# Each column block of the up projection reads its weight parts from another place inside 512 bytes

## The chip, the cores and the metric

The kernel runs on one core of a Trainium2 chip. The metric is device time in microseconds (us) of one execution. Engines are named as the profile names them: PE is TensorE's matrix multiply, PEld its loading of the stationary operand, DVE is VectorE, ACT is ScalarE, POOL is GpSimd, and SP issues most of the DMAs.

## What is computed

One decoder layer over 256 tokens of width 2048: a combined input projection, two parallel branches (a gated DeltaNet and a block-sparse attention), an output projection, and then a gated MLP with a causal convolution of width 3 behind its up projection. The change touches the up projection, `h @ w_up`, alone:

```python
D_MODEL = 2048
SEQ = 256
D_FF = 5632
...
    x = x + merged @ w_out[l]
    h = rms_norm(x, ln2[l])
    u = causal_dwconv(h @ w_up[l], ffn_conv[l], ffn_conv_bias[l])
    u_gate, u_val = jnp.split(u, 2, axis=-1)
    x = x + (jax.nn.silu(u_gate) * u_val) @ w_down[l]
return rms_norm(x, final_norm)
```

## The kernel before

**Split arithmetic.** All large products are made in a 32-bit format of TensorE called fp32r here, with each operand split into a high and a low part. For a weight tile, ACT casts the float32 original `wraw` to the high part `wh` (line 108, in `split`), and DVE subtracts it from the original to get the low part `wl` (line 105, in `low`). The activations are split once in the same way. Three products are kept: high by high, low by high and high by low.

**Weight buffers.** `fetch` (line 116) has SP load one 1 MB piece of weights, 128 partitions by 2048 float32, into one of four `wraw` buffers. `load_w` (line 125) makes both parts of it in two pieces of 1024 columns each. `parts` (line 121) hands out the buffers `wh` and `wl`, two of each. Each is 2048 + 128 elements wide, and its argument `o` says at which element the 2048 that are used begin. With `o` at 0 a part starts at the buffer's own start. `SHIFT` (line 30) is 72 elements, 288 bytes.

**Two kinds of product.** `chunk` and `block` (lines 160 to 180) use the weights as the stationary operand and the activations as the moving one; they serve the DeltaNet's projections (`ps_gdn`) and the output projection (`ps_wo`, whose activations `mc` are shifted by `SHIFT` too), with `o` at 0. `by_token` (line 182) does it the other way round: a 128 by 128 block of the activations is the stationary operand, loaded before each matmul, and 512 columns of `wh` or `wl` are the moving operand. It serves `ps_z`, `ps_v`, `ps_moba`, `ps_gate`, `ps_br` and the up projection, `ps_up`, all with `parts(SHIFT)`. The down projection (`pd`, line 987) also moves the weights, with `o` at 0; its last two weight pieces lie in the tile `tail` (line 985), which takes the memory that `hc` and `h2` had.

**The up projection** (line 964) goes over 22 blocks of 512 columns. Each block loads four pieces of weights, and each piece feeds 24 matmuls of 512 columns: two halves of the tokens, four slices of the contraction, three products. That is 96 matmuls for a block and 2112 for the stage. The stationary operand is `h2`, the normed activations, in the memory of the tile tagged `hc`. Behind each block, ACT moves the sums out of PSUM (line 968), and the transposing and convolving of it (`convolved`, line 943) is done in small steps between the matmuls of the blocks that follow.

**Addresses.** In the built program each `wraw`, `wh` and `wl` buffer begins 192 bytes past a multiple of 512, in every partition, and so do the down projection's activation parts `ah` and `al`. `hc`, `h2` and `tail` begin 480 bytes past one. Blocks and slices inside these tiles are multiples of 512 bytes apart, so the place inside 512 bytes is the same for each matmul of a stage. With `SHIFT` the moving operand of the up projection begins at 192 + 288 = 480.

Of the kernel before, what the change touches and what calls it, by code (L numbers as in the profile page):

```python
# [22 lines left out]
KD = D // P  # L23
# [4 lines left out]
EPS = 1e-6  # L28
EVERY = 1700
SHIFT = 72  # L30
ATT_SCALE = 128 ** -0.5
CONST_FIELDS = [
    ("ident", 128), ("nm", 128), ("my", 2 * 64), ("nm3", 3 * 128), ("invf", 16),
# [37 lines left out]
def layer_kernel(ctx: ExitStack, tc: tile.TileContext, xT, pos, cst, ceye, vec, convw, ffw, bdv,  # L71
# [8 lines left out]
    def r3(t, b):  # L80
        return t.rearrange("p (a b) -> p a b", b=b)
# [15 lines left out]
    def main_mm(ps, a, b, start, stop):  # L97
        pe.matmul(ps, a, b, start=start, stop=stop, skip_group_check=True)  # L98
        spent[0] += 215 if b.free_size() > T else 108
        if spent[0] >= EVERY:  # L100
            spent[0] = 0
            tick()
# [4 lines left out]
    def split(hi, lo, src):  # L107
        casts.append(act.copy(hi, src))  # L108
        return low(hi, lo, src)
# [6 lines left out]
    def fetch(src, n=2048):  # L116
        raw = wpool.tile([P, 2048], F32, name="wraw", tag="wraw", bufs=4)
        sp.dma_start(raw[:, :n], src)
        return raw

    def parts(o=0):

        return [wpool.tile([P, 2048 + 128], F32R, name=t, tag=t)[:, o:o + 2048] for t in ("wh", "wl")]

    def load_w(src, n=2048, into=None, piece=1024, raw=None):
        raw = raw or fetch(src, n)
        wh, wl = into or parts()
        for o in range(0, n, piece):
            lows.append(split(wh[:, o:o + piece], wl[:, o:o + piece], raw[:, o:o + piece]))
        return wh[:, :n], wl[:, :n]  # L130
# [23 lines left out]
    def mmt(name):  # L154
        return pst[0].tile([P, 2, 2, T] if wide[0] else [P, 2, T], F32, name=name, tag="mm")
# [15 lines left out]
    def chunk(blocks, x, kt, name, raws=(None, None), piece=1024, steps=((0, 0, None), (1, 0, None)), flush=None):  # L171
        ps = mmt("ps_" + name)
        ws = {}
        for n, (j, k0, k1) in enumerate(steps):
            while n == flush and bg:
                tick()
            if j not in ws:
                ws[j] = load_w(blocks[j], kt * P, raw=raws[j], piece=piece)
            block(ps[:, j], ws[j], x, kt, k0, k1)
        return ps  # L180

    def by_token(ws, x, kt, name):

        if wide[0]:
            t = mmt(name)
            ps = [t[:, i].rearrange("p a b -> p (a b)") for i in range(2)]
        else:
            ps = [mmt(name).rearrange("p a b -> p (a b)") for _ in range(2)]
        for q_ in range(kt // 4):
            wh, wl = (r3(t, 512) for t in load_w(ws[q_], into=parts(SHIFT)))  # L190
            for i in range(2):
                s = slice(i * P, (i + 1) * P)
                for k in range(4):
                    a = q_ * 4 + k
                    main_mm(ps[i], x[:, a, 0, s], wh[:, k, :], a == 0, False)
                    main_mm(ps[i], x[:, a, 1, s], wh[:, k, :], False, False)
                    main_mm(ps[i], x[:, a, 0, s], wl[:, k, :], False, a == kt - 1)
        return ps
# [476 lines left out]
    def pair(w, i):  # L675
        return [w[2 * i], w[2 * i + 1]]

    def z_gates(n):
        ps = by_token(w_z[4 * n:4 * n + 4], hc, KD, "ps_z")
        zv = ya[:, 4 * n:4 * n + 4, :].rearrange("p (a b) c -> p a b c", b=2)  # L680
        for i in range(2):
            act.activation(zv[:, :, i, :], r3(ps[i], T), AF.Silu, scale=cols[:, 5 + i, 0:1])

    v4 = []
    for n in range(2):
# [4 lines left out]
        for pr in range(2):  # L690
# [3 lines left out]
            for a, t in enumerate((kq[:, 1], kq[:, 0], v)):  # L694
                if gr == 0 and a < 2:
                    ps = (ps_q0, ps_k0)[a]
                else:
                    ps = chunk(pair(w_gdn, 3 * gr + a), hc, KD, "gdn")
# [9 lines left out]
        if n == 0:  # L708
            bg.append(rotary())

            for c in range(2):
                ps = by_token(w_mv[4 * c:4 * c + 4], hc, KD, "ps_v")
                v4.append(m.tile([P, 2, 2 * T], F32, name="v_"))
                for i in range(2):
                    act.mul(v4[c][:, i, :], ps[i], cols[:, 5 + i, 0:1])
# [18 lines left out]
    def moba(h0, q, k, v):  # L734
        ss = []
        for j in range(2):
# [8 lines left out]
            dve.tensor_reduce(mx[:, 1:2], s_[:, T:], axis=AX.X, op=ALU.max)  # L745
            dve.tensor_scalar(mx[:, 0:2], mx[:, 0:2], -ATT_SCALE, None, op0=ALU.mult)
            act.activation(s_[:, :T], s_[:, :T], AF.Exp, bias=mx[:, 0:1], scale=ATT_SCALE, accum_out=mx[:, 2:3])
            act.activation(s_[:, T:], s_[:, T:], AF.Exp, bias=mx[:, 1:2], scale=ATT_SCALE, accum_out=mx[:, 3:4])
            dve.reciprocal(mx[:, 2:4], mx[:, 2:4])
# [35 lines left out]
    for n in range(2):  # L785
        if n:
            while ("pair", 1, 1) not in done:
                tick()
            gdn_st.close()
            mq = mq_st.enter_context(tc.tile_pool(name="mq", bufs=1, reuse_waits="tile"))  # L790
        qks.append([])
        for a in range(2):
            ps = by_token(w_moba[8 * n + 4 * a:8 * n + 4 * a + 4], hc, KD, "ps_moba")
            t = (m if a else mq).tile([P, 4, 2, P], F32, name=f"qk{a}", bufs=1)
            for i in range(2):
                act.activation(t[:, :, i, :], r3(ps[i], P), AF.Identity, scale=cols[:, 5 + i, 0:1])
            qks[n].append(t)
            bg.append(rotated(t, ("qk", n, a)))

    gts = []  # L800
    for c in range(8):
        ps = by_token(w_gate[4 * c:4 * c + 4], hc, KD, "ps_gate")
# [28 lines left out]
    m = m_st.enter_context(tc.tile_pool(name="mp", bufs=1, reuse_waits="tile"))  # L831
    mc = m.tile([P, KD * 2 * T + 128], F32R, name="mc")[:, SHIFT:SHIFT + KD * 2 * T].rearrange("p (k a t) -> p k a t", a=2, t=T)

# [32 lines left out]
    for c in range(4):  # L866
        ps = by_token(w_ba[2 * c:2 * c + 2], yc[0], H, "ps_br")
# [3 lines left out]
        ps = by_token(w_bb[2 * c:2 * c + 2], yc[1], H, "ps_br")  # L871
# [15 lines left out]
    h2 = hp.tile([P, KD, 2, T], F32R, name="h2", tag="hc")  # L887
    for c in range(8):
        if c == 0:
            steps = ((0, 0, 8), (0, 8, 12), (1, 0, 4), (0, 12, KD), (1, 4, KD))  # L890
            ps = chunk(pair(w_o, c), mc, KD, "wo", steps=steps, flush=1)
# [5 lines left out]
        else:  # L897
            ps = chunk(pair(w_o, c), mc, KD, "wo")
# [44 lines left out]
    def convolved(n, ut):  # L943
        c, val = n // 2, n % 2
        uc = ub.tile([P, 4, T], F32, name="uc", bufs=2)
        yield from turn(r3(uc.rearrange("p k t -> p (k t)"), P), ut.rearrange("p k i c -> p (k i c)"),
                        ub.tile([P, 8, P], F32, name="xt"), sp, 4, 1)
        yield from wait(5)
        if not val:
            gates[c] = ub.tile([P, 4, T], F32, name="sgt", bufs=2)  # L950
        for k in range(4):
            ch = 4 * c + k
            if val:
                t = ub.tile([P, T], F32, name="cvf", bufs=2)
                conv3(t, uc[:, k, :], NF + ch)
                pool.tensor_tensor(acts[:, ch, :], gates[c][:, k, :], t, op=ALU.mult)  # L956
            else:
                conv3(gates[c][:, k, :], uc[:, k, :], ch)
            yield
        if not val:  # L960
            act.activation(gates[c], gates[c], AF.Silu)

    bg.append(residual_turned())
    for n in range(NF // 2):
        ps = by_token(w_up[4 * ((n % 2) * 11 + n // 2):][:4], h2, KD, "ps_up")
        ut = ub.tile([P, 4, 2, P], F32, name="ut", bufs=2)
        for i in range(2):
            act.activation(ut[:, :, i, :], r3(ps[i], P), AF.Identity, scale=R2c[:, i:i + 1])
        bg.append(convolved(n, ut))
# [14 lines left out]
    wl = {}  # L984
# [8 lines left out]
    for k in range(NF):  # L993
# [10 lines left out]
        wh, wl_ = load_w(w_dn[k], into=[tail[:, t, k - NF + 2, :] for t in range(2)] if k >= NF - 2 else None)  # L1004
# [98 lines left out]
```

## Time and profile before

| | |
|---|---|
| median of three runs (lowest, highest) | 1464.84 us (1463.58, 1468.98) |
| span of the profiled execution, first to last instruction | 1464.6 us |
| mean granted TensorE clock | 0.998 |
| up projection: first to last matmul of `ps_up` | 731.9 to 1214.2 us |
| down projection: first to last matmul of `pd` | 1214.4 to 1456.5 us |
| bytes moved by DMA in the span | 297.43 MB |
| landing of one 1 MB piece of `w_up`, median | 7.4 us |

The page of the profile has the busy time of each engine, the span in 40 slices, the chain of work that ended last and the costliest groups of instructions. In a group's row stand the line, the engine, the operation, the tiles written and read, the shapes and the count, then its busy time and the mean length of one in ns, then the idle time of the engine ahead of it and what ended that. Matmuls overlap: the length of one runs from its start to its modelled end, and the next begins before that. The distance from one start to the next is read from the timeline. Rows of the tiles `ps_up`, `pd` and `ps_wo` belong to the stages named above, since a tile's name is that of its stage.

### The profile page before, as it was taken

To read this page: it belongs to the slowest core of one execution; us is meant where nothing else is said; L and a number is where in the kernel's file an instruction comes from. 1 tells how busy PE (TensorE), PEld (TensorE's weight loads), DVE (VectorE), ACT (ScalarE), POOL (GpSimd) and SP (SyncE) were. 2 spreads that over 40 slices of the span, in tenths; PEclk is the share of its full clock that TensorE was granted. 3 is DMA by queue.
4 is the path that set the end of the run, shared out by engine and by line. 5 is a ranking of instruction groups with operands and counts; after the bars stand their busy time and mean duration, and the time that the engine had idled before them with its cause. 6 is when DMAs were issued, how large, how long until landed. Compare 5 with 4: busy or idle time off the path is not lost.

```text
span 1464.6 us, 19064 instructions
## 1 busy us (share of the span) xinstructions
PE 1449.5 (99%) x7193; PEld 1228.0 (84%) x7193; DVE 957.7 (65%) x1358; ACT 737.1 (50%) x944; POOL 132.5 (9%) x121
## 2 busy tenths in 40 slices
PE   8999999999999999999999999999999999999997
PEld 8898899888887888888888888888888887888886
DVE  7987876888455445767656576576676666654554
ACT  5665444645375434445446455455455555444444
POOL 0011000200003000001100122210011111000000
PEclk9999999999999999999999999999999999999999
DMA  9566554577535555676557677777687776555552
GB/s 323 175 217 213 181 190 142 151 238 238 185 117 187 196 184 200 210 266 229 181 173 235 172 252 223 191 252 226 183 255 219 211 229 218 204 199 198 183 194 86
DMA packets 206252, 297.43 MB, mean 203 GB/s; under 512 B 167272, under 2 KB 169712, under 8 KB 174032
## 3 DMA queue, kind: packets, MB, share of 16 engines
q1 hardware_dynamic: 185952, 288.27, 60.4%
q10 hardware_dynamic: 18128, 4.20, 1.5%
q0 software_dynamic: 2080, 3.75, 0.7%
q8 instruction: 56, 0.92, 0.3%
q14 instruction: 36, 0.29, 0.1%
HBM read 273.54 MB, written 3.15 MB: 189 GB/s over the span
## 4 chain that ended last, share of the span: by engine, by line
PE 73%; DMA 11%; SPq 7%; DVE 6%; ACT 1%; issue 1%; POOLq 0%; ACTq 0%; DVEq 0%; POOL 0%
PE pd L98 16%; PE ps_gate L98 11%; PE ps_up L98 10%; PE ps_gdn L98 8%; DMA wraw<-in_w_up 8%; SPq L464 7%; PE ps_wo L98 6%; PE ps_moba L98 6%; PE ps_br L98 6%; DVE wl L105 3%; PE ps_z L98 3%; PE ps_v L98 3%; DMA uc<-xt 2%; DVE sgt L939 2%; DMA wraw<-in_w_gdn 1%
## 5 line engine op out<-in xcount | busy, mean ns | idle before, releaser
L105 DVE TENSOR_TENSOR wl<-wraw,wh 128x1024 fp32r<-128x1024 f32 x496 | 603.0, 1251 | 278.2 <-ACT wh L108 277.8
L108 ACT CAST wh<-wraw 128x1024 fp32r<-128x1024 f32 x496 | 495.3, 1046 | 423.3 <-PE ps_up L98 139.8
L98 PE MATMUL ps_up<-wh,h 128*128 128x512 f32 x1408 | 433.8, 389 | 0.0
L98 PEld LDWEIGHTS ps_up<-wh,h 128*128 128x128 f32 x1408 | 264.3, 188 | 54.5
L98 PE MATMUL ps_up<-wl,h 128*128 128x512 f32 x704 | 275.0, 391 | 0.3 <-DVE wl L105 0.2
L98 PE MATMUL ps_gate<-wh,hc 128*128 128x512 f32 x512 | 158.4, 394 | 1.3 <-ACT wh L108 1.3
L98 PEld LDWEIGHTS ps_up<-wl,h 128*128 128x128 f32 x704 | 132.1, 188 | 30.8 <-DVE wl L105 3.2
L98 PE MATMUL pd<-wl,ah 128*128 128x512 f32 x336 | 129.7, 390 | 0.5 <-DVE wl L105 0.5
L98 PE MATMUL pd<-wh,al 128*128 128x512 f32 x336 | 129.2, 389 | 0.0
L98 PE MATMUL ps_gdn<-hc,wh 128*128 128x256 f32 x704 | 125.6, 281 | 0.0
L98 PEld LDWEIGHTS ps_gate<-wh,hc 128*128 128x128 f32 x512 | 96.5, 189 | 21.3 <-ACT wh L108 1.7
L956 POOL TENSOR_TENSOR acts<-sgt,cvf 128x256 f32<-128x256 f32 x44 | 68.7, 1579 | 451.6 <-ACT wh L108 284.4
L98 PEld LDWEIGHTS ps_gdn<-hc,wh 128*128 128x128 f32 x704 | 108.0, 188 | 0.3
L98 PE MATMUL ps_gdn<-hc,wl 128*128 128x256 f32 x352 | 98.6, 280 | 0.7 <-DVE wl L105 0.7
L98 PE MATMUL ps_gate<-wl,hc 128*128 128x512 f32 x256 | 98.3, 394 | 0.4 <-DVE wl L105 0.4
L98 PE MATMUL pd<-wh,ah 128*128 128x512 f32 x336 | 93.0, 390 | 0.5 <-DVE pd L981 0.4
L98 PE MATMUL ps_wo<-mc,wh 128*128 128x512 f32 x256 | 89.2, 391 | 0.2 <-DVE mc L864 0.2
L98 PE MATMUL ps_moba<-wh,hc 128*128 128x512 f32 x256 | 77.8, 390 | 0.0
L98 PEld LDWEIGHTS pd<-wh,ah 128*128 128x128 f32 x336 | 62.9, 188 | 14.8 <-ACT wh L108 0.9
L98 PEld LDWEIGHTS pd<-wl,ah 128*128 128x128 f32 x336 | 63.1, 188 | 14.0 <-DVE wl L105 0.9
L98 PEld LDWEIGHTS pd<-wh,al 128*128 128x128 f32 x336 | 63.1, 188 | 13.1
L108 ACT CAST ah<-acts 128x256 fp32r<-128x256 f32 x44 | 17.7, 406 | 109.5 <-PE pd L98 104.4
(428 smaller groups left out, 1704.9 us busy)
## 6 DMA issues: line engine op xcount, KB each, us to landing
wraw<-in_w_up SPq DMA_DIRECT2D x88, 1024.0 KB, 7.4
wraw<-in_w_dn SPq DMA_DIRECT2D x44, 1024.0 KB, 4.9
wraw<-in_w_gate SPq DMA_DIRECT2D x32, 1024.0 KB, 5.0
wraw<-in_w_gdn SPq DMA_DIRECT2D x22, 1024.0 KB, 5.0
wraw<-in_w_moba SPq DMA_DIRECT2D x16, 1024.0 KB, 5.6
wraw<-in_w_o SPq DMA_DIRECT2D x16, 1024.0 KB, 5.5
uc<-xt SPq DMA_DIRECT2D x352, 32.0 KB, 2.0
wraw<-in_w_z SPq DMA_DIRECT2D x8, 1024.0 KB, 6.4
```

The lines of the kernel that those rows point to most:

```text
L98: pe.matmul(ps, a, b, start=start, stop=stop, skip_group_check=True)
L105: return (eng or dve).tensor_tensor(lo, src, hi.bitcast(F32), op=ALU.subtract)
L108: casts.append(act.copy(hi, src))
L464: eng.dma_start(dst[32 * e:32 * e + 32, :, 32 * a:32 * a + 32], xt[32 * a:32 * a + 32, :, 32 * e:32 * e + 32])
L939: dve.scalar_tensor_tensor(t[:, d:], u[:, :T - d], w[:, 2 - d:3 - d], t[:, d:], op0=ALU.mult, op1=ALU.add)
L956: pool.tensor_tensor(acts[:, ch, :], gates[c][:, k, :], t, op=ALU.mult)
```

## The change

A table `PLACES` of 22 shifts replaces the one shift of 72 elements in the up projection: block `n` takes entry `n`. The first sixteen are multiples of 8 elements (32 bytes) from 0 to 120, that is, each place in steps of 32 bytes inside 512 once; the last six are 2, 4, 70, 74, 76 and 12 elements (8, 16, 280, 296, 304 and 48 bytes). Entry 9 is 72, as before. All other uses of `by_token` keep `SHIFT`.

```diff
 SHIFT = 72
+PLACES = (0, 8, 16, 24, 32, 40, 48, 56, 64, 72, 80, 88, 96, 104, 112, 120, 2, 4, 70, 74, 76, 12)
...
-    def by_token(ws, x, kt, name):
+    def by_token(ws, x, kt, name, shift=SHIFT):
...
-            wh, wl = (r3(t, 512) for t in load_w(ws[q_], into=parts(SHIFT)))
+            wh, wl = (r3(t, 512) for t in load_w(ws[q_], into=parts(shift)))
...
-        ps = by_token(w_up[4 * ((n % 2) * 11 + n // 2):][:4], h2, KD, "ps_up")
+        ps = by_token(w_up[4 * ((n % 2) * 11 + n // 2):][:4], h2, KD, "ps_up", PLACES[n])
```

The order of instructions on every engine, what each of them waits for, and the base address of every buffer are the same in both built programs. What differs is the address at which ACT and DVE write, DVE reads and TensorE reads the parts of the weights in the up projection, and, from line 31 on, the line numbers by one.

## The prediction

> **What bounds the kernel now.** I read the page first: the busy shares, the slices, the chain that ended last and the costliest groups.
>
> ```profile
> PE 1449.5 (99%) x7193; PEld 1228.0 (84%) x7193; DVE 957.7 (65%) x1358; ACT 737.1 (50%) x944; POOL 132.5 (9%) x121
> PE   8999999999999999999999999999999999999997
> PEclk9999999999999999999999999999999999999999
> PE 73%; DMA 11%; SPq 7%; DVE 6%; ACT 1%; issue 1%; POOLq 0%; ACTq 0%; DVEq 0%; POOL 0%
> L105 DVE TENSOR_TENSOR wl<-wraw,wh 128x1024 fp32r<-128x1024 f32 x496 | 603.0, 1251 | 278.2 <-ACT wh L108 277.8
> L108 ACT CAST wh<-wraw 128x1024 fp32r<-128x1024 f32 x496 | 495.3, 1046 | 423.3 <-PE ps_up L98 139.8
> ```
>
> TensorE is busy for 99% of the span at a full granted clock, and the engines that prepare its weights wait for it: ACT's cast sits idle 139.8 us until a ps_up matmul frees a buffer. So the span is set by how often TensorE can start a matmul. Then I asked for the stage that the change touches: the instructions on the tile ps_up, the waits of TensorE between 732 and 1214 us, and the sums of that stretch.
>
> ```profile
> L98 PE MATMUL ps_up<-wh,h x1408: 387/389/475, 731.9 to 1214.0; 128*128 128x512 f32 x176
> L98 PE MATMUL ps_up<-wl,h x704: 387/389/505, 732.5 to 1214.2; 128*128 128x512 f32 x176
> PE ps_up L98 <- DVE wl L105: 0.2, 1, 0.2
> 732.00:1214.00 482.00, 481.67 (x2122) 396.65 (x2122) 316.58 (x373) 256.20 (x320) 62.11 (x40) 1.00 0.72 216
> ```
>
> The up projection is 1408 + 704 = 2112 matmuls of 512 columns between 731.9 and 1214.2 us, 482.3 us, a third of the span. TensorE waits 0.2 us in it for anything the profile names. Here each nanosecond per matmul is worth 2.1 us, nearly all of it on the path.
>
> The durations (389 ns) overlap, so what counts is the distance from start to start. It is read from the timeline of TensorE: its columns are start in us, length in us, and how many were merged into the row.
>
> ```profile
> 1100.13 0.39 PE L98 MATMUL ps_up<-wl,h 128*128 128x512 f32 x1
> 1100.36 0.62 PE L98 MATMUL ps_up<-wh,h 128*128 128x512 f32 x2
> ...
> 1104.89 0.39 PE L98 MATMUL ps_up<-wl,h 128*128 128x512 f32 x1
> ```
>
> From 1100.13 to 1104.89 lie 21 starts: 4.76 / 21 = 226.7 ns. 2112 of these make 478.7 us, so all but 3.6 us of the stage is this one steady step. It isn't the only step that the same instructions at the same addresses take. Just after a short wait it is another:
>
> ```profile
> 1074.46 0.64 PE L98 MATMUL ps_up<-wh,h 128*128 128x512 f32 x2
> 1074.93 0.40 PE L98 MATMUL ps_up<-wl,h 128*128 128x512 f32 x1
> 1075.16 0.62 PE L98 MATMUL ps_up<-wh,h 128*128 128x512 f32 x2
> ...
> 1077.24 0.62 PE L98 MATMUL ps_up<-wh,h 128*128 128x512 f32 x2
> ```
>
> From 1074.46 to 1077.24 are 12 starts in 2.78 us, 231.7 ns each; then the 226.7 sets in. So a stream of matmuls settles after a disturbance, and before it has settled a matmul costs 5.0 ns more. The change asks whether the place of the moving operand decides about this.
>
> **The change, part by part.** No instruction is added, removed or reordered on any engine, and no wait and no DMA; the buffers keep their base addresses and size. What moves is the start of wh and wl inside their padded buffers, in the up projection alone. The built program has all of these buffers 192 bytes past a multiple of 512, and h2, which TensorE loads as the stationary operand, 480 past. With 72 elements (288 bytes) the moving operand starts at 480 too: **the same place inside 512 bytes as the stationary one**. After the change that holds for block 9 alone. Blocks 18, 19 and 20 (70, 74, 76) lie 8 to 16 bytes from it, and the other 18 blocks 32 to 256 bytes, counted round the 512.
>
> *ACT and DVE, which write and read at the new places.* Two stages of the trace have these buffers at 192 and at 480: the down projection (first two rows) and the branch projections (last two).
>
> ```profile
> L105 DVE TENSOR_TENSOR wl<-wraw,wh 128x1024 fp32r<-128x1024 f32 x55 | 65.0, 1221 | 14.8 <-ACT wh L108 14.8
> L108 ACT CAST wh<-wraw 128x1024 fp32r<-128x1024 f32 x56 | 56.0, 1047 | 0.0
> L105 DVE TENSOR_TENSOR wl<-wraw,wh 128x1024 fp32r<-128x1024 f32 x26 | 30.9, 1218 | 17.4 <-ACT wh L108 17.4
> L108 ACT CAST wh<-wraw 128x1024 fp32r<-128x1024 f32 x26 | 26.0, 1047 | 42.0 <-PE ps_br L98 42.0
> ```
>
> 1221 against 1218 ns and 1047 against 1047 ns: their place costs nothing. The cover is large as well: a load feeds 24 matmuls, 24 x 226.7 = 5.44 us, against two DVE pieces of 1.22 and two casts of 1.05. At 8 bytes past a 16 (places 2, 70 and 74) no row shows them; even doubled they fit (4.9 of 5.44 us). I cost it at nothing; without that cover, three blocks of four loads would lose at most what DVE takes beyond 5.44 us.
>
> *TensorE.* What the trace has of a moving and a stationary operand at different places are two stages, both with the moving one at 480 and the stationary one at 192, 288 bytes apart. The first is the end of the down projection, where the tile tail takes turns with wh and wl (which lie at 192):
>
> ```profile
> 1441.49 0.63 PE L98 MATMUL pd<-tail,ah 128*128 128x512 f32 x2
> ...
> 1442.89 0.39 PE L98 MATMUL pd<-wl,ah 128*128 128x512 f32 x1
> ...
> 1443.36 0.62 PE L98 MATMUL pd<-tail,ah 128*128 128x512 f32 x2
> ...
> 1444.75 0.40 PE L98 MATMUL pd<-wl,ah 128*128 128x512 f32 x1
> ...
> 1445.21 0.62 PE L98 MATMUL pd<-tail,ah 128*128 128x512 f32 x2
> ...
> 1446.61 0.40 PE L98 MATMUL pd<-wl,ah 128*128 128x512 f32 x1
> ```
>
> Six tail matmuls (rows of 2, 1, 2 and 1) take 1.40, 1.39 and 1.40 us: 4.19 / 18 = 232.8 ns, 6.1 over the settled step. The second is the output projection, which alternates 512 and 256 columns:
>
> ```profile
> 679.81 0.39 PE L98 MATMUL ps_wo<-mc,wh 128*128 128x512 f32 x1
> 680.04 0.28 PE L98 MATMUL ps_wo<-mc,wl 128*128 128x256 f32 x1
> ...
> 683.97 0.39 PE L98 MATMUL ps_wo<-mc,wh 128*128 128x512 f32 x1
> ```
>
> Twelve pairs in 4.16 us: 346.7 ns, 120.0 more than one settled 512-column matmul. If a column costs 0.417 ns and each matmul 13.3 ns besides (0.417 x 512 + 13.3 = 226.7), the pair comes to 0.417 x 768 + 26.7 = 346.7: no loss at all. So the two nearest rows bound the cost of a place that doesn't match at **0 and +6.1 ns**. Below zero the bound comes from a stream that reloads its weights as often and shows no such surplus, the plain f32 matmuls near the start:
>
> ```profile
> 15.20 4.05 PE L261 MATMUL ps_gdn<-xs,wraw 128*128 128x256 f32 x18
> 10.85 3.69 PE L261 MATMUL ps_gdn<-xs,wraw 128*128 128x256 f32 x16 [0.15 <-DVE hc L214]
> L261 PE MATMUL ps_gdn<-xs,wraw 128*128 128x256 f32 x64 | 14.8, 384 | 2.1 <-DMA xs<-in_xT 1.9 <-DVE hc L214 0.2
> ```
>
> (4.05 - 0.38) / 17 = 215.9 ns from start to start, with 384 ns for the last one: a lower end of -10.8 ns, for another number format, so far off.
>
> I take +5.0 ns, the step of the stream that hasn't settled. The tail is the nearest row (same columns, format and line), but each of its runs is six long and begins with a change of place, while a settling takes about a dozen; its 232.8 may be a little too high for a block of 96. For the three places within 16 bytes of 72 I take nothing. **Sum: 18 blocks x 96 matmuls x 5.0 ns = 8.6 us.** The chance waits of DVE (part of the 3.6 us) are as likely to grow as to shrink with a slower TensorE. The profiled span is 1464.6 us and the median of the three runs 1464.84, so the two can be taken as one: 1464.84 + 8.6 = **1473.5 us**, +0.6%.
>
> **The rivals.**
>
> *The place makes no difference; not slower.* Mechanism: the step is a matter of time alone. It settles whenever moving and stationary reads come in a fixed rhythm, wherever they lie. For it: the output projection, 288 bytes apart and without loss; and in the down projection both operands lie at 192, at 480 in the up projection, with the same settled step. The tail would then be slow because its moving operand jumps between 192 and 480, not because it stands apart from ah. Each block would pay one settling at most, 2.78 - 12 x 0.2267 = 0.06 us, 21 times 1.3: 1464.8 to 1466.1. It decides if settled blocks appear at 32 to 256 bytes of distance. The Trainium skill's page "TensorE: Matmul & The Clock Gate", section "What happens when you issue a matmul", gives this rival a reason: TensorE reads the moving operand and the weights through two ports of their own, and loading the next weights takes nothing from the running matmul. By it the sum would be nothing, 1464.8; the tail's 232.8 beside 226.7 speaks against it, the output projection's 346.7 for it.
>
> *Some places settle and some don't.* If half of the 18 find the 226.7 again: 9 x 96 x 5.0 = 4.3 us, 1469.1.
>
> *They settle, but on a slower step.* Nothing says that a settled step must be the fast one. At the tail's +6.1 for the 18: 1728 x 6.1 = 10.5 us, 1475.4; if the near ones go too, 2016 x 6.1 = 12.3, 1477.1. The slowest steps in the unsettled stretch, 1074.46 to 1075.16, three in 0.70 us (233.3 ns, +6.6), would give 13.4 us for 21 blocks, 1478.2. Unaligned places could be worse still.
>
> *Some places are better.* A quarter of the 21 blocks at 215.9: 5 x 96 x 10.8 = 5.2 us less, 1459.6; all of them, 1443. No 512-column fp32r stretch quoted here settles below 226.7, so this has little.
>
> *The shift might not reach the matmuls.* The built program has the moving operand's starts at 192, 224, ... 160, 200, 208, 472, 488, 496 and 240 inside 512, as the table says: excluded.
>
> **How the numbers follow.** Forecast 0.42; no difference 0.26; a slower settled step 0.15; half of the places 0.12; better places 0.05. A measurement of this kernel can tell about 0.5%, 7.3 us, from no change; slower begins at 1472.2. The forecast's 1473.5 stands just above it: with 15 blocks in place of 18, or 4 ns, it falls below, so I put 0.30 of its 0.42 on slower and 0.12 on the same. The slower step gives slower 0.15 and half of the places 0.03; the same gets 0.12 + 0.26 + 0.09 = 0.47; slower 0.48; faster 0.05. The range runs from just below no change, 1464.0, to 1481.0, where the slower step at 21 blocks and a worse place or two still fit; below lie the better places, above blocks at 240 ns and more.
>
> **What would show it.** The up projection's stage (482.3 us now) should take about 491, and everything else should keep its length. Within it block 9 should step at 226.7, 18 to 20 about the same, and the other blocks between 231 and 233 with uneven steps. Settled blocks at 226.7 all over show the first rival right; even steps of 233 the slower settling; a block under 226 the better places. The forecast fails if distance to the stationary operand isn't what counts. If DVE or ACT rows of the up stage lengthen at the finer places and TensorE waits for them, I was wrong to cost them at nothing.

## The result, and the profile after

The changed kernel takes 1472.2 us (median of 7 runs, 1471.32 to 1473.56), the kernel before 1464.84 (7 runs, 1460.63 to 1468.98): 7.4 us more by the medians. The ratio is **1.0055 (95% interval 1.004 to 1.0071)**, that is, 8.1 us: small, but clear of the noise. The profiled execution took 1472.73 us with a span of 1471.0, so some 1.7 us of a time lie outside the span.

The page of the changed kernel, the rows that answer to those of before (its line numbers are higher by one):

```profile
PE 1456.9 (99%) x7193; PEld 1228.1 (83%) x7193; DVE 957.5 (65%) x1358; ACT 737.8 (50%) x944; POOL 122.0 (8%) x121
PEclk9999999999999999999999999999999999999999
PE 90%; DVE 4%; SPq 2%; DMA 1%; issue 1%; ACT 1%; POOLq 0%; DVEq 0%; POOL 0%; ACTq 0%
L106 DVE TENSOR_TENSOR wl<-wraw,wh 128x1024 fp32r<-128x1024 f32 x496 | 602.8, 1251 | 321.7 <-ACT wh L109 321.1
L109 ACT CAST wh<-wraw 128x1024 fp32r<-128x1024 f32 x496 | 495.4, 1046 | 477.0 <-PE ps_up L99 199.0
```

TensorE is at 99% and at full clock as before. DVE and ACT take what they took (1251 and 1046 ns), so the new places cost them nothing; what changed for them is that they wait longer for TensorE: the cast's idle time behind ps_up grew from 139.8 to 199.0 us. TensorE's share of the chain went from 73% to 90%: it is more alone in setting the end.

The tile ps_up of the changed kernel, and the sums of its stage and of the down projection's:

```profile
L99 PE MATMUL ps_up<-wh,h x1408: 388/394/478, 730.9 to 1222.2; 128*128 128x512 f32 x176
L99 PE MATMUL ps_up<-wl,h x704: 388/394/483, 731.5 to 1222.4; 128*128 128x512 f32 x176
730.90:1222.70 491.80, 491.80 (x2126) 398.52 (x2125) 315.08 (x374) 257.09 (x321) 50.92 (x40) 1.00 0.71 214
1222.70:1462.90 240.20, 240.13 (x1057) 197.89 (x1055) 136.15 (x159) 110.16 (x152) 6.55 (x4) 1.00 0.54 184
```

From its first start to its last (730.9 to 1222.4) the up projection takes 491.5 us after 482.3, 9.2 more. The down projection takes 240.2 after 242.1 (1214.4 to 1456.5). This execution also reached the up projection 1.0 us sooner (at 730.9, before at 731.9), and its span grew by 6.4 only.

Each block now has its own step. These are pairs of rows from TensorE's timeline of the changed kernel, a start early and a start late in one block; the matmul on `wl` is each third one, so the number of starts between two rows is the difference over three steps:

```profile
745.19 0.40 PE L99 MATMUL ps_up<-wl,h 128*128 128x512 f32 x1
...
749.39 0.40 PE L99 MATMUL ps_up<-wl,h 128*128 128x512 f32 x1
...
767.91 0.39 PE L99 MATMUL ps_up<-wl,h 128*128 128x512 f32 x1
...
772.67 0.39 PE L99 MATMUL ps_up<-wl,h 128*128 128x512 f32 x1
...
812.21 0.39 PE L99 MATMUL ps_up<-wl,h 128*128 128x512 f32 x1
...
816.33 0.39 PE L99 MATMUL ps_up<-wl,h 128*128 128x512 f32 x1
...
946.13 0.39 PE L99 MATMUL ps_up<-wl,h 128*128 128x512 f32 x1
...
950.21 0.39 PE L99 MATMUL ps_up<-wl,h 128*128 128x512 f32 x1
...
1170.25 0.40 PE L99 MATMUL ps_up<-wl,h 128*128 128x512 f32 x1
...
1174.45 0.40 PE L99 MATMUL ps_up<-wl,h 128*128 128x512 f32 x1
```

Block 0 (place 192): 4.20 us for 18 starts, 233.3 ns. Block 1 (place 224): 4.76 for 21, **226.7**. Block 3 (288): 4.12 for 18, 228.9. Block 9 (480, as before): 4.08 for 18, **226.7**. Block 19 (488, 8 bytes from block 9's): 4.20 for 18, 233.3. The mean of each block's last 36 steps, by distance, is in the table further down. Two things stand out: the sixteen places in steps of 32 bytes repeat after 256 bytes, step for step, and the good place of block 9 has a bad one 8 bytes beside it.

### The profile page after: what moved, and what is told of

Same layout as the page of the kernel before. It is cut to its first block, busy times and chain, and to the rows that moved or that the text cites. A ratio compares the mean times of both kernels' runs of the same rounds, so it can differ in the third digit from the quotient of the medians.

```text
span 1471.0 us, 19064 instructions
## 1 busy us (share of the span) xinstructions
PE 1456.9 (99%) x7193; PEld 1228.1 (83%) x7193; DVE 957.5 (65%) x1358; ACT 737.8 (50%) x944; POOL 122.0 (8%) x121
## 4 chain that ended last, share of the span: by engine, by line
PE 90%; DVE 4%; SPq 2%; DMA 1%; issue 1%; ACT 1%; POOLq 0%; DVEq 0%; POOL 0%; ACTq 0%
PE ps_up L99 33%; PE pd L99 14%; PE ps_gate L99 10%; PE ps_gdn L99 6%; PE ps_wo L99 6%; PE ps_moba L99 6%; PE ps_br L99 6%; PE ps_v L99 3%; SPq L465 2%; DVE wl L106 2%; PE ps_z L99 1%; DMA wraw<-in_w_gdn 1%; PE pu L626 0%; PE py L620 0%; PE g L87 0%
## 5 line engine op out<-in xcount | busy, mean ns | idle before, releaser
L106 DVE TENSOR_TENSOR wl<-wraw,wh 128x1024 fp32r<-128x1024 f32 x496 | 602.8, 1251 | 321.7 <-ACT wh L109 321.1
L109 ACT CAST wh<-wraw 128x1024 fp32r<-128x1024 f32 x496 | 495.4, 1046 | 477.0 <-PE ps_up L99 199.0
L99 PE MATMUL ps_up<-wh,h 128*128 128x512 f32 x1408 | 441.2, 394 | 0.0
L957 POOL TENSOR_TENSOR acts<-sgt,cvf 128x256 f32<-128x256 f32 x44 | 57.5, 1325 | 470.2 <-DVE cvf L940 385.2
```

Source lines behind the costliest of these rows:

```text
L106: return (eng or dve).tensor_tensor(lo, src, hi.bitcast(F32), op=ALU.subtract)
```

## Experiments

**The map moved with the stationary operand.** In the changed kernel only the moving operand changes its place, so its own place and its distance from `h2` can't be told apart. Here `h2` begins 64 bytes further on; `hc` in the same memory stays where it was, and as the tile grows by 512 bytes, nothing else changes its place inside 512:

```diff
-    hc = hp.tile([P, KD, 2, T], F32R, name="hc", tag="hc")
+    hc = hp.tile([P, KD * 2 * T + 128], F32R, name="hc", tag="hc")[:, 128:].rearrange("p (k a t) -> p k a t", a=2, t=T)
...
-    h2 = hp.tile([P, KD, 2, T], F32R, name="h2", tag="hc")
+    h2 = hp.tile([P, KD * 2 * T + 128], F32R, name="h2", tag="hc")[:, 16:16 + KD * 2 * T].rearrange("p (k a t) -> p k a t", a=2, t=T)
```

> The changed kernel with h2, the stationary operand of the up projection, begun 64 bytes further on (at 32 inside 512 in place of 480); the moving places are those of the change. If the distance from the stationary to the moving operand decides, counted modulo 256 bytes, the map moves along by 64 bytes: the settled 226.7 ns leaves the blocks at 224 and 480 and appears at 32 and 288, 228.9 goes from 32 and 288 to 96 and 352, 234.2 from 128 and 384 to 192 and 448, and block 9 (480) steps at 233.3. If the moving operand's own place decides, the map stays where it is: 226.7 at 224 and 480, 228.9 at 32 and 288. The whole time is about that of the change in both cases, 1470 to 1474 us.

It took 1472.07 us in its one run. Its timeline in block 9 (480), whose step had been 226.7, and in block 11 (32), which had stepped at 228.9:

```profile
932.18 0.40 PE L99 MATMUL ps_up<-wl,h 128*128 128x512 f32 x1
...
936.38 0.40 PE L99 MATMUL ps_up<-wl,h 128*128 128x512 f32 x1
...
976.96 0.39 PE L99 MATMUL ps_up<-wl,h 128*128 128x512 f32 x1
...
980.36 0.39 PE L99 MATMUL ps_up<-wl,h 128*128 128x512 f32 x1
```

4.20 us for 18 starts in block 9, 233.3; 3.40 for 15 in block 11, 226.7. All sixteen places in steps of 32 bytes moved along: 226.7 at 32 and 288, 228.9 at 96 and 352, 234.3 at 192 and 448. ACT and DVE wrote and read at the same places as in the changed kernel, so they aren't the cause; neither is the moving operand's own place. **What decides in this stage is the distance from the stationary to the moving operand, modulo 256 bytes.** Distances below are counted so, from the start of the stationary operand forward.

**A finer map**, with 22 other distances in the table:

```diff
-PLACES = (0, 8, 16, 24, 32, 40, 48, 56, 64, 72, 80, 88, 96, 104, 112, 120, 2, 4, 70, 74, 76, 12)
+PLACES = (78, 82, 84, 86, 90, 92, 94, 98, 100, 102, 106, 108, 110, 114, 116, 118, 58, 60, 62, 73, 7, 75)
```

> The changed kernel with 22 other places: distances to the stationary operand of 24, 40, 48, 56, 72, 80, 88, 104, 112, 120, 136, 144, 152, 168, 176, 184, 200, 208, 216, 4, 252 and 12 bytes, modulo 256. If the match to the stationary operand is the best there is, no block settles under 226.7 ns and most lie between 229 and 237: the up projection takes 488 to 495 us, the kernel 1470 to 1477. If the steps at 228.9 (64 bytes) and 230.0 (248 bytes) are flanks of better places, some of these blocks settle below 226.7, down to 220.0, the next step 6.67 ns lower.

It took 1473.04 us in its one run. The slowest block, 120 bytes from `h2`, and the only one at 226.7, 252 bytes (that is, 4 bytes before `h2`'s place):

```profile
944.63 0.40 PE L99 MATMUL ps_up<-wl,h 128*128 128x512 f32 x1
...
949.67 0.40 PE L99 MATMUL ps_up<-wl,h 128*128 128x512 f32 x1
...
1194.25 0.39 PE L99 MATMUL ps_up<-wl,h 128*128 128x512 f32 x1
...
1198.33 0.39 PE L99 MATMUL ps_up<-wl,h 128*128 128x512 f32 x1
```

5.04 us for 21 starts, 240.0 ns; 4.08 for 18, 226.7. No block settled below 226.7, as expected if the match is the best there is. The map of all three kernels, where a distance that came twice gave the same within 0.2 ns:

| distance mod 256, bytes | settled step, ns |
|---|---|
| 0, 252 | 226.7 |
| 12, 64 | 228.9 |
| 56, 104, 248 | 230.0 |
| 80, 112 | 231.1 |
| 16 | 231.7 |
| 8, 24, 32, 40, 48, 88, 96, 128, 136, 144, 168, 176, 184, 192, 200, 224, 232 | 233.3 |
| 152 | 233.4 |
| 160, 216, 208 | 234.3, 234.4, 234.7 |
| 72 | 235.6 |
| 4, 240 | 236.7 |
| 120 | 240.0 |

**All blocks at one slow place**, to weigh the step against the time; this line stands in place of the change's list:

```diff
+PLACES = (112,) * 22
```

> All 22 blocks at 160 bytes from the stationary operand (shift 112 elements), the slowest of the 32-byte places: 234.2 ns in the changed kernel. If TensorE's step alone makes the time, the up projection takes 2112 x 234.2 = 494.6 us, 12.3 more than before, less any chance waits that a slower TensorE hides: 1474 to 1478 us, DVE and ACT rows as before. If part of the change's 7.4 us came from the new places meeting between blocks (each block begins at another place), this kernel has no such change and loses less than the step says: under 1473 us.

It took 1475.91 us (6 runs); the ratio to the kernel before is 1.0075 (1.0052 to 1.0098), that is, 11.0 us, as the first expectation had it. Two starts of its timeline:

```profile
999.79 0.40 PE L99 MATMUL ps_up<-wl,h 128*128 128x512 f32 x1
...
1009.63 0.40 PE L99 MATMUL ps_up<-wl,h 128*128 128x512 f32 x1
```

9.84 us for 42 starts, 234.3 ns, and so in the whole stage. The meeting of places between blocks costs next to nothing: in the changed kernel, which has it, the settled steps of all blocks come to 490.5 us of the stage's 491.5, and about 1 us goes to ten small matmuls of the tile `R` in block 0, which the kernel before has too. But here the step alone is 2112 x (234.3 - 226.7) = 16.1 us over a stage without waits, and the time grew by 11.0. The second kernel for this has one of the smallest steps above 226.7:

```diff
+PLACES = (88,) * 22
```

> All 22 blocks at 64 bytes from the stationary operand (shift 88 elements), where the changed kernel settled at 228.9 ns, 2.22 more than at no distance. The step alone makes 2112 x 2.22 = 4.7 us: 1468 to 1469.5 us if nothing is given back. If the slower TensorE hides the waits for DVE and ACT that the kernel before has in its up and down projections (3.2 and 2.7 us by its weight-load rows), most of the 4.7 us is given back: 1464 to 1466.5 us, and those wait rows fall under 1.5 us in the profile.

It took 1465.73 us (11 runs), a ratio of **1.0007 (0.9995 to 1.0019)**: 1.0 us, where the step makes 4.7. Most of it was given back, as the second expectation had it. The waits of TensorE's weight loads in the kernel before from 700 us on, longest first; behind the colon stand us in total, times, and the longest:

```profile
PEld ps_up L98 <- DVE wl L105: 3.2, 8, 0.6
PEld pd L98 <- ACT wh L108: 0.9, 2, 0.5
PEld pd L98 <- DVE wl L105: 0.9, 1, 0.9
PEld pd L98 <- DVE pd L981: 0.9, 1, 0.9
```

And the same view of this kernel:

```profile
PEld ps_up L99 <- DVE wl L106: 0.5, 2, 0.3
PEld pd L99 <- DVE pd L982: 0.2, 1, 0.2
```

5.9 us of waits became 0.7. One profile of each is thin evidence, since such waits differ from one execution to the next, and the execution profiled here was the fastest of its 11. But the three kernels at the end of this section leave the up projection at no distance, and their profiles (the rows are those of 192 bytes, the first list and the finer list, in this order) have these rows:

```profile
PEld ps_up L98 <- DVE wl L105: 1.1, 3, 0.5
...
PEld ps_up L99 <- DVE wl L106: 4.3, 7, 1.9
PEld ps_up L99 <- ACT wh L109: 0.9, 1, 0.9
...
PEld ps_up L99 <- DVE wl L106: 4.7, 4, 1.9
PEld ps_up L99 <- ACT wh L109: 1.7, 2, 1.0
```

Four profiles with the fast step wait 3.2, 1.1, 5.2 and 6.4 us in the up projection, 4.0 on average. The five with slower steps (the changed kernel, `h2` moved, the finer map and the two of one place) wait 0, 0, 0, 0 and 0.5. So a slower step gives back some 4 us of waits, and only what goes beyond counts. That DVE and ACT then finish early enough is the likely reason; no run sets their speed alone. The down projection, whose step didn't change, also waits less in these five (0 to 0.5 us) than in three of the four others (2.6 to 3.2, but 0.2 in the fourth); why is not shown.

**Weights that stand.** In the DeltaNet's and the output projection the weights are loaded and the activations move. A list of places for their chunks, in the kernel before:

```diff
+STILL = [0, 8, 16, 24, 32, 40, 48, 56, 4, 6, 12, 0, 8, 16, 24, 32, 40, 48, 56]
...
-                ws[j] = load_w(blocks[j], kt * P, raw=raws[j], piece=piece)
+                ws[j] = load_w(blocks[j], kt * P, into=parts(place), raw=raws[j], piece=piece)
```

> The kernel before, with the place of the weights varied where they are the stationary operand and the activations move: shifts of 0, 8, 16, 24, 32, 40, 48, 56, 4, 6 and 12 elements in the eleven DeltaNet chunks, 0, 8, ... 56 in the eight of the output projection. If the distance matters there too, the mean steps of the chunks differ by 3 ns or more: the DeltaNet chunks (116.8 ns at 32 bytes before) spread over 113 to 120, the pairs of the output projection (346.7 at 32 bytes) over 340 to 360. If the length of the stationary operand's load hides it at 256 columns, the DeltaNet chunks stay at 116 to 118 all over. The whole time stays within 5 us of the kernel before.

In these stages the activations move at 480 and the weights stand at 192 plus the shift, so a shift of 0 is a distance of 32 bytes, one of 8 elements (32 bytes) is no distance, and 24 elements are 192. Distance matters here too. The DeltaNet chunk at no distance (first pair), and the one at 192 bytes:

```profile
40.00 0.28 PE L99 MATMUL ps_gdn<-hc,wl 128*128 128x256 f32 x1
...
45.76 0.28 PE L99 MATMUL ps_gdn<-hc,wl 128*128 128x256 f32 x1
...
87.22 0.28 PE L99 MATMUL ps_gdn<-hc,wl 128*128 128x256 f32 x1
...
94.70 0.28 PE L99 MATMUL ps_gdn<-hc,wl 128*128 128x256 f32 x1
```

5.76 us for 48 starts, 120.0 ns, which 96, 128 and 160 bytes have too, and no chunk settled slower; 7.48 for 66, 113.3, the best; 116.7 at 32 as before. So the map for 256 columns is another than that for 512: no distance, the best there, is among the worst here. The pairs of the output projection settled on 346.7 ns at 32 and 160 bytes and on 348.9 to 353.3 elsewhere. These are nine pairs at no distance:

```profile
659.89 0.40 PE L99 MATMUL ps_wo<-mc,wh 128*128 128x512 f32 x1
...
663.07 0.40 PE L99 MATMUL ps_wo<-mc,wh 128*128 128x512 f32 x1
```

3.18 us, 353.3 ns a pair. The whole took 1470.21 us in its one run, 6 us above the median before; the time lies just outside what I expected. By its profile the up projection, which this kernel leaves alone, took 485.6 us after 482.3, with the 5.2 us of waits above.

A finer list, for neighbours of 192 (`STILL = [23, 25, 22, 26, 28, 20, 18, 30, 21, 27, 60, 4, 6, 30, 34, 60, 28, 2, 36]`):

> As the map of standing weights (the DeltaNet chunks 113.3 ns at 192 bytes, 116.7 at 32 and 120.0 at 0; pairs of the output projection 346.7 at 32 and 160), with finer distances: 196, 188, 200, 184, 176, 208, 216, 168, 204, 180 and 48 bytes in the DeltaNet chunks, 16, 8, 168, 152, 48, 176, 24 and 144 in the output projection. If 113.3 is one step of a ladder of 6.67 ns with more below it, a neighbour of 192 lies under 113.3 (the next step would be 106.7); if the load of the stationary operand bounds it (small f32 matmuls step at 111 to 112 ns), none lies under 111, and the neighbours lie between 112 and 121. Pairs under 346.7 would show that the output projection can gain; otherwise they lie between 347 and 354.

It took 1467.06 us in its one run. Nothing settled below 113.3: the chunks at 168, 180 and 204 bytes reach it in long stretches, those at 184, 188 and 200 settled on 117.8 to 118.3, the rest on 116.7 to 120.0. The pairs settled on 349.4 to 353.3; none beats 346.7.

**A version meant to beat both**: the kernel before with all DeltaNet weights at 192 bytes.

```diff
-                ws[j] = load_w(blocks[j], kt * P, raw=raws[j], piece=piece)
+                ws[j] = load_w(blocks[j], kt * P, into=parts(24 if name == "gdn" else 0), raw=raws[j], piece=piece)
```

> The kernel before (up projection at no distance) with the standing weights of the eleven DeltaNet chunks begun 24 elements further on, so that the moving activations lie 192 bytes past them, where the map settled at 113.3 ns in place of 116.7. 11 x 96 = 1056 matmuls at 3.33 ns less make 3.5 us: a ratio of 0.9976, and the DeltaNet chunks at 113 to 114 ns. If the time there is set by something else between the chunks (the preparing of weights, the branches' own work), the steps fall and the waits of TensorE in that stage grow, and the ratio stays within 0.999 to 1.001.

It missed: 1464.5 us (12 runs), ratio 0.9994 (0.9978 to 1.001). Its timeline shows why, early in the stage (first pair) and further on:

```profile
27.30 0.28 PE L98 MATMUL ps_gdn<-hc,wl 128*128 128x256 f32 x1
...
31.72 0.28 PE L98 MATMUL ps_gdn<-hc,wl 128*128 128x256 f32 x1
...
95.31 0.28 PE L98 MATMUL ps_gdn<-hc,wl 128*128 128x256 f32 x1
...
100.96 0.28 PE L98 MATMUL ps_gdn<-hc,wl 128*128 128x256 f32 x1
```

4.42 us for 39 starts, 113.3 ns; 5.65 for 48, 117.7. The same distance settles on one of two steps, and six of the eleven chunks ran at the slower one nearly throughout. The ratio is the one of the second expectation, but not its reason, and neither foresaw two steps. The kernel before has this too, at 32 bytes: most of its chunks step at 116.7 ns, the first and the last at 117.8. What picks the step after a disturbance wasn't tried.

## Why the prediction was right, and where it wasn't

**The number** was 1473.5, measured 1472.2, and slower was forecast; of the 8.6 us forecast, 8.1 came (7.4 by the medians). What it rests on was right: the lever, and that distance from the stationary operand decides. Three terms were off and partly cancel, so that it came this close is in part luck.

**What bounds the kernel** held: the loss is in TensorE's step from start to start, in the up projection, and 2112 steps of it are the lever. ACT and DVE at the new places cost nothing, as costed, down to 8 and, in the finer map, 4 bytes.

**That distance from the stationary operand decides** held, against the rival that the place makes no difference. Moving `h2` settled it. The argument for that rival from the output projection rested on an accident of its distance: 32 and 160 bytes are the two where its pairs take 346.7 ns; at no distance they take 353.3. The sum that made 346.7 a pair without loss takes 120.0 ns for 256 columns and 226.7 for 512; both are the steps at no distance, and yet a pair there takes 6.6 more, so a mixed pair is not the sum of two streams. Its 0.417 ns a column stands on no row beside the two that it was to judge. That page of the Trainium skill, "TensorE: Matmul & The Clock Gate", section "What happens when you issue a matmul", says that loading the next weights takes no read bandwidth from the running matmul. Here the move of `h2`, which in this stage only the weight loads read, changed block 9's step from 226.7 to 233.3 ns, so in this kernel the two reads are not independent in time. Whether the load holds up the matmul or the matmul the load, no run shows.

**"Misplaced blocks don't settle" failed.** I took the step of the unsettled stretch, +5.0 ns. They do settle, as the third rival had it: within a dozen matmuls each runs an even step or a short cycle of steps, most with a mean of 233.3. The tail of the down projection, which I set aside as a little too high, was the right row: it is 32 bytes from its stationary operand modulo 256, and its 232.8 ns is near the 233.3 that the map has there. Nor is each distance bad: block 1, 256 bytes away, is as good as block 9, since 256 bytes count as none. Over the 18 blocks the mean, block 1 among them, is 232.7, +6.0 ns: 1728 x 6.0 = 10.4 us in place of 8.6.

**"Nothing for the three near places" failed.** They cost 3.3, 6.7 and 5.0 ns, 1.4 us together. Together the steps make 11.8 us.

**"The chance waits are as likely to grow as to shrink" failed.** They shrank: by the ratios, 11.8 us of steps became 8.1 of time, 16.1 became 11.0, 4.7 became 1.0. That about 4 us are given back (3.7 to 5.1, each with 2 to 3 us of noise to either side) is shown by the three kernels; that these are the waits behind DVE and ACT is borne out by the rows of nine profiles. I had read the wait of TensorE's matmuls (0.2 us) and not that of its weight loads (3.2 us in the up projection, 2.7 in the down projection), which stand on an engine row of their own.

**The base.** I set the profiled span equal to the median. With some 1.7 us around the span, that execution of the kernel before took about 1466.3 us, 1.5 above the median. This costs the forecast nothing, as its sum starts from the median. The lower end of the prices, -10.8 ns, came from 256-column matmuls of another format; no distance of the map settled below 226.7.

## What to carry to other kernels

Where a matmul stream is the bound, read the distance from start to start, not the length of a matmul, and look whether it is the same in stages of one form: a difference with no wait beside it can come from where the two operands lie to each other. Here 512-column fp32r matmuls wanted the moving operand at the stationary one's place modulo 256 bytes, and all other distances tried but one (252 bytes) cost 1 to 6%. With 256 columns, or with the two in turn, the best distance was another, so the map is to be measured for the form at hand. Before pricing a slower bound, add the waits of all its rows, those of the weight loads too: a kernel that just keeps pace gives part of the loss back.

## What the runs showed of the hardware

The settled steps of the up projection fall on a ladder of 6.67 ns: 226.7 is 34 rungs, 233.3 is 35 and 240.0 is 36, and 113.3 with 256 columns is 17. The steps between come to whole rungs over two to seven matmuls (230.0 makes 69 rungs in two, 228.9 makes 103 in three). So TensorE's start seems to be tied to a beat of 6.67 ns; that is a pattern in the numbers, and its cause wasn't shown. The pattern of distances repeats after 256 bytes, and is not smooth inside it: 12 bytes cost 2.2 ns, 4 bytes 10.0 and 252 bytes nothing. One distance can have two settled steps (113.3 and 117.7 ns at 192 bytes with 256 columns). Why it repeats after 256 bytes, and whether the load that counts is the matmul's own or the next one's, stays open: in all these stages both have the same place.
